# A hybrid decoder layer on Trainium2: the second output projection without gate/up products inside it

## The chip, the cores and the metric

The kernel runs on one core of a Trainium2 chip. The core has a matrix engine (TensorE, PE in the profile), a vector engine (VectorE, DVE), a scalar engine (ScalarE, ACT), a general engine (GpSimd, POOL) and a sync engine (SyncE, SP) that here issues most of the DMAs. TensorE multiplies a stationary operand of 128 by 128 with a moving one of up to 128 by 512 and writes into banks of an accumulation memory; the other engines read these banks. The metric is the device time of one execution in microseconds (us). The profile is one execution taken by the hardware profiler.

## What is computed

One decoder layer on 2048 tokens of 1024 channels. Cut to what matters here:

```python
hn = rms_norm(h, mix_pre_g)
proj = hn @ w_in                       # 1024 x 1792: conv input u, k, v, q
attn_out = sliding_window_attention(q, k, v, attn_sinks, rel_bias)   # window 128
conv_out = conformer_conv(u, ...)      # GLU, 31 causal taps, LayerNorm, silu, @ w_conv_pw
mixed = concatenate([attn_out, conv_out], axis=-1) @ w_out
h = h + rms_norm(mixed, mix_post_g)
hn = rms_norm(h, ffn_pre_g)
ff = (silu(hn @ w_gate) * (hn @ w_up)) @ w_down    # 1024 -> 2816 -> 1024
out = h + rms_norm(ff, ffn_post_g)
```

All inputs and outputs are float32. A product of two float32 matrices is made of three matmuls: each operand is split into a high part and a low part (the rest), and high by high, high by low and low by high are added up in one bank.

## The kernel before

**Tiles and stages.** The tokens go in four tiles of 512, numbered 0 to 3. A letter and a number name a stage, and every buffer's name carries it after an @ (without the number in the profile): A is the input projection of a tile, B its attention in four blocks of 128 tokens, C its convolution (taps on VectorE, then a tail: LayerNorm, silu and the pointwise product), W its output projection and norms. The feed-forward part works on pairs of tiles, (0, 1) and (2, 3), with a seven-product scheme of sums and differences: H makes the operands of a pair, F the gate and up products, G the down projection.

**Lanes and the planning clock.** The program is written out by a main stream and several lanes. Each stage is a generator that yields planned microseconds; `run` (line 1353) walks the main stage, adds what it yields to the planning clock `clk` and lets each lane issue as much work as its rate allows. A lane's item may have a condition (`needs`), tested on each pump, and items of one lane follow one another. `until` issues the rest of a lane's items up to a name at once. What is issued in this way has a priority in that order; the tile framework's scheduler then sets the order of the instructions on each engine, so that a later instruction can be placed ahead of an earlier one that is not ready. Lane `lc` issues the convolution taps at a lower priority and at a planned rate (0.4 for tile 2, 0.1 for tile 3 during F, 0.9 during G), `ld` the convolution tails of tiles 0 and 1, `lb` attention, `lh` the H stage.

**The output projection** (`stage_w`, line 697). The eight rows of `mixT` (0 to 3 from attention, 4 to 7 from the convolution) are taken in four groups of two. For a group, `acts` loads the two rows into buffers `at` (two of them) and splits them into `hl` (eight); for each half of the 1024 output columns, `weight` loads two blocks of `w_out` into `raw` (two buffers), splits them on ScalarE, and loads the low parts from `lo_out`, where the first projection has stored them. `block_half` (line 671) then does four banks of six matmuls each, planned at 1.3 us a bank, and adds each bank into `acc` (buffers `mid` for tile 1). So a group is 48 matmuls and W1 is 192. At the end `norm_w` (line 747) makes the residual, the norms, and the rows `hn_scr`; for tile 1 it is given to lane `lh` under the name N1.

**The stop in the second one.** W1 is run as the main stream with `ready=...`: after its second group (rows 2 and 3) it goes through the first `Q0` = 8 products of the F stage (`stage_pre`, line 887, with q from 0 to 7). Half-way, at the fifth, it issues the rest of tile 1's convolution tail (`ld.until("C1")`) and the operands of its third group. Each product is 12 matmuls of a 128-row block of w_gate or w_up with the operand B11 (tiles `x`), planned at 2.76 us; its result is stored to `keeps`. After W1, `stage_pre` goes on with q = 8 to 39: q = 8 to 19 with B11, and 20 to 39 with B21 on top of the kept results, which are loaded into `gb` (two buffers) and put into a bank by ScalarE (line 924) before the product.

**The first pair's operands.** `stage_h_plain` (line 829) makes B11 and B21 of a pair, four tiles each: a load of 512 tokens by 128 channels from `hn_scr`, four transposes on TensorE, scaling on ScalarE into `gb`, a store to `hT`, and the split. Before, both are put into `lh` without a condition as W1 starts, so they are issued beside its first half. `stage_pre` issues what is missing itself (line 935). S0 (`stage_h_sums`, line 842) makes the other operands from both tiles of the pair; it is gated by product 22 and the end of attention, and the taps are held until it has been issued.

Of the kernel before, what the change touches and what calls it, by code (L numbers as in the profile page):

```python
# [28 lines left out]
KC = D // P  # L29
# [8 lines left out]
def layer_kernel(ctx, tc, x, xT, cols, rows, sinks, relb, onehot, w_in, w_pw, w_out, w_gate, w_up, w_down, out):  # L38
# [8 lines left out]
    lab = ["X0"]  # L47
# [10 lines left out]
    def f4(tag, shape=(P, D)):  # L58
        return t_(tag, shape)

    def f2(tag, shape=(P, T)):
        return t_(tag, shape)

    def hl(tag):
        return t_(tag, (P, 2, T), F32R)
# [5 lines left out]
    def bank(tag, bufs):  # L71
        return ps.tile([P, T], F32, tag=tag, name=nm(tag), bufs=bufs)

    mm = lambda: bank("mm", 4)
# [65 lines left out]
    def weight(src, low, made, raw=None, on_pool=True):  # L140
        if raw is None:
            raw = t_("raw", (P, 2, T))
            nc.sync.dma_start(raw, src)
        return [split_w(raw[:, n], "w", low[n], made, on_pool) for n in range(2)]
# [526 lines left out]
    def block_half(acc, units, n, first, L, bank_of, s0=0):  # L671
        cs = slice(n * T, (n + 1) * T)
        for i in range(len(acc)):
            s = i + s0
            lab[0] = L
            o = bank_of()
            three(o, [((a[s // 4][:, 0, ss(s)], a[s // 4][:, 1, ss(s)]), (w[:, 0], w[:, 1])) for a, w in units])
            if first:
                act(acc[i][:, cs], o, AF.Copy)  # L679
            else:  # L680
                vtt(acc[i][:, cs], acc[i][:, cs], o, ALU.add)
            yield 0.65 * len(units)
# [11 lines left out]
            cs = slice(n * T, (n + 1) * T)  # L694
            tied(stt(acc[:, cs], acc[:, cs], r, gb[n], ALU.mult, ALU.mult))

    def stage_w(w, spill, G, atag, htag, mtag, bank_of, norm=None, ready=None):
        L = f"W{w}"
        lab[0] = L
        acc = [f4(atag) for _ in range(4)]  # L700

        def acts(gi, ms=None):
            aa = []
            for m in ms or load(gi):
                a = hl(htag)
                act(a[:, 0], m, AF.Copy)  # L706
                vtt(a[:, 1], m, a[:, 0].bitcast(F32), ALU.subtract)
                aa.append([a])
            return aa

        def load(gi):
            ms = []
            for c in range(G * gi, G * gi + G):
                ms.append(f2(mtag))
                nc.sync.dma_start(ms[-1], mixT[c, :, w * T : (w + 1) * T])
            return ms

        first = load(0)
        if w != 1:
            yield 5.0  # L720
            lab[0] = L
        nxt = acts(0, first)
        for gi in range(KC // G):
            aa = nxt
            for n in range(2):
                lab[0] = L
                if n == 0 and w != 1 and gi + 1 < KC // G:
                    rows_next = load(gi + 1)
                if n == 1 and gi + 1 < KC // G and not (ready and G * gi + G == 4):
                    nxt = acts(gi + 1, rows_next if w != 1 else None)  # L730
                ws = weight(w_out[2 * gi : 2 * gi + 2, :, n * T : (n + 1) * T].rearrange("c p t -> p c t"),
                            lo_out[n, 2 * gi : 2 * gi + 2], w > 0)
                yield from block_half(acc, list(zip(aa, ws)), n, gi == 0, L, bank_of)
            if ready and G * gi + G == 4:
                for i, c in enumerate(ready()):
                    if i == Q0 // 2:
                        ld.until("C1")
                        lab[0] = L
                        nxt = acts(gi + 1)
                    yield c  # L740
        tail = norm_w(w, spill, acc, mtag)
        if norm:
            norm(tail)
        else:
            yield from tail
# [54 lines left out]
    def lo(x, w, on_pool):  # L800
        (ptt if on_pool else vtt)(w[:, 1], x, w[:, 0].bitcast(F32), ALU.subtract)
# [9 lines left out]
    def turned(w, k, bank_of, tag):  # L811
        c = load_cols(w, k, tag)
        b = bank_of()
        for s in range(4):
            nc.tensor.transpose(b[:, s * P : (s + 1) * P], c[:, s], ident)
        return b
# [12 lines left out]
    def stage_h_plain(ws, ops, n, off):  # L829
        L = f"H{ws[0]}"  # L830
        for k in range(4):
            lab[0] = L
            b = turned(ws[0], k + off, tr, COLTAG[ws[0]][k] if ws[0] else "fa")
            u = f2("gb")
            act(u, b, AF.Copy, scale=g_ffn[:, k + off : k + off + 1])
            nc.scalar.dma_start(hT[ws[0] // 2][k + off], u)
            o = op_tile(ws, ops, n, k, {})
            act(o[:, 0], u, AF.Copy)
            lo(u, o, False)
            yield 2.0  # L840
# [46 lines left out]
    def stage_pre(ws, ops, mid, keep, q0=0, q1=None):  # L887
        PRE = PRES[ws[0]]
        q1 = q1 or 2 * PRE
        L = f"F{ws[0]}"  # L890
        raws = {}
        wops = {}
        kept = {}

        def load(q):
            if q < q1 and q % 2 == 0:
                lab[0] = L
                half, m = divmod(q, PRE)
                raw = t_("raw", (P, 2, T))
                for j in range(2):  # L900
                    src, pr = MATS[m + j]
                    nc.sync.dma_start(raw[:, j], src[2 * pr][:, half * T : (half + 1) * T])
                    raws[q + j] = raw[:, j]

        def fetch(q):
            if PRE <= q < q1:
                lab[0] = L
                kept[q] = f2("gb")
                nc.sync.dma_start(kept[q], keep[q - PRE])

        def split(q):
            if q < q1:
                lab[0] = L
                raw = raws.pop(q)
                wops[q] = split_f(raw, hl("w"))
                lo(raw, wops[q], ws[0] and q % 2 == 1)

        seeded = {}

        def seed(q):  # L920
            if PRE <= q < q1:
                lab[0] = L
                seeded[q] = mm()
                act(seeded[q], kept.pop(q), AF.Copy)  # L924

        load(q0)
        load(q0 + 2)
        for q in range(q0, q0 + 3):
            split(q)
        for q in range(q0, q1):  # L930
            half, m = divmod(q, PRE)
            started.add(f"P{ws[0]}.{q}")
            bn = "B21" if half else "B11"
            if len(ops.get(bn, ())) < 4:
                lh.until(f"{bn}.{ws[0]}")
            split(q + 3)
            load(q + 4)
            fetch(q + 2)
            lab[0] = L
            seed(q + 1)  # L940
            lab[0] = L
            o = seeded.pop(q) if half else mm()
            product(o, wops.pop(q), ops[bn], not half)
            if not half:
                u = f2("fa")
                act(u, o, AF.Copy)
                nc.scalar.dma_start(keep[m], u)
            else:
                if MATS[m][0] is w_gate:
                    sg = f2("fa")  # L950
                    act(sg, o, AF.Silu)
                else:
                    vtt(sg, sg, o, ALU.mult)
                    nc.sync.dma_start(mid[0, MATS[m][1]], sg)
            yield 2.76
# [316 lines left out]
    def since(lane, name, dt):  # L1272
        return name in lane.done and clk[0] >= lane.done[name] + dt
# [60 lines left out]
    NS = 12  # L1334
    AHEAD = 3
    PRES = {0: 20, 2: 16}
    Q0 = 8
    POOL_LO = (3, 6)
    PRE_S0, PRE_S2 = 22, 16
    H1, H2, H3, H4 = 0, 4, 7, 11  # L1340
    lb = Lane(RB, 0)
    lc = Lane(RC0, LC)
    lw = Lane(RW0, 0)
    lf = Lane(1.2, 0)
    lh = Lane(1.2, 0)
    lt = Lane(RT, 0)
    ld = Lane(2.0, 0)
# [5 lines left out]
    def run(gen):  # L1353
        for c in gen:
            clk[0] += c
            for lane in lanes:
                lane.pump(c)
# [53 lines left out]
    mids = [dr.tile([7, NF // 2, P, T], F32, name=f"mids{i}") for i in range(2)]  # L1411
    hT = [dr.tile([KC, P, T], F32, name=f"hT{i}") for i in range(2)]
    td = dr.tile([4, NF // 2, P, T], F32, name="td")
    keeps = [dr.tile([PRES[2 * i], P, T], F32, name=f"keeps{i}") for i in range(2)]
    ws, ops = (0, 1), {}
    for n, off in (("B11", 0), ("B21", 4)):
        lh.add(n + ".0", stage_h_plain(ws, ops, n, off))
    run(stage_w(1, True, 2, "mid", "hl", "at", mm, norm=lambda g: lh.add("N1", g), ready=lambda: stage_pre(ws, ops, mids[0], keeps[0], 0, Q0)))
    lc.hold = lambda: "S0" not in lh.done
    lh.until("B21.0")  # L1420
    lh.add("S0", stage_h_sums(ws, ops), lambda: f"P0.{PRE_S0}" in started and "B3" in lb.done)
    run(stage_pre(ws, ops, mids[0], keeps[0], Q0))
    lt.add("TS", stage_tsums(td))
    run(stage_p1(ws, ops, mids[0], keeps[0]))
    lt.until("TS")
# [2 lines left out]
    ws, ops = (2, 3), {}  # L1428
# [76 lines left out]
```

## Time and profile before

| what | value |
|---|---|
| three timed runs | 2012.16, 2020.62, 2017.57 us; median 2017.57 |
| span of the profiled execution, first to last instruction | 2016.4 us |
| granted TensorE clock, mean over the span | 0.991 |
| TensorE busy / VectorE busy / ScalarE busy | 1957.8 / 1489.5 / 985.7 us |
| HBM read and written | 330.60 MB and 119.02 MB |
| chain that ended last: TensorE / DMA / VectorE / ScalarE / issue | 38% / 5% / 3% / 1% / 1% of the span |

Only the instructions themselves lie in the span; the profiled execution's own time is not given beside it, so the span is compared with the median of the timed runs, which is 1.2 us longer. Busy time on TensorE counts pipelined matmuls whose ends are modelled: a matmul alone is listed at some 390 ns, and in a full stream the next begins 0.228 us later. In the rows of the timeline, the first two numbers are start and duration in us, then engine, line, operation, the tile written and the tiles read, shape and count; the bracket is the idle time of the engine just before, and what ended it. In the rows of windows, each engine has its busy time and in parentheses its instructions, then come the granted clock, the mean busy share of the DMA engines and GB/s. Helpers record many operations under one line (108 for matmuls, 85 for VectorE), so the names of the tiles tell the stages apart. In the rows of DMA issues, the size in KB of one and its median time from issue to landing end the row.

### The profile page before, as it was taken

The page shows a single profiled execution, that of the slowest core. Times are in us where ns is not written, and L with a number is a line of the kernel's source. Part 1 is how long each engine was busy: PE and PEld are TensorE (multiplying, and loading weights), DVE is VectorE, ACT ScalarE, POOL GpSimd, SP SyncE. Part 2 cuts the span into 40 slices and gives each one's busy share as a digit, 9 for nine tenths or more (in the row PEclk, how much of TensorE's full clock was granted, in tenths as well). Part 3 has the DMA queues.
Part 4 walks back from the last instruction along what each step waited for, and adds up shares of the span by engine and source line. Part 5 has one row for each costly group of instructions (what it writes and reads, how often), then busy time and mean ns, then how long its engine had stood idle before and what let it go on. Part 6 is the DMA issues. An engine that isn't in the chain of part 4 may idle for free. (4 is left out here: it accounts for less than half of the span.)

```text
span 2016.4 us, 27154 instructions
## 1 busy us (share of the span) xinstructions
PE 1957.8 (97%) x8826; PEld 1563.3 (78%) x8826; DVE 1489.5 (74%) x2679; ACT 985.7 (49%) x1938; POOL 355.0 (18%) x415
## 2 busy tenths in 40 slices
PE   8999999999998999999989999999899999999998
PEld 7877767677667778888878878778688888888886
DVE  5998987985794899888569984475766765545558
ACT  5455455457546633333355466456643343345543
POOL 6000223322110300000001022103523332221000
PEclk9999999999999999999989999999999999999999
DMA  8786645669559878777476778579944443366654
GB/s 309 267 298 221 207 148 175 194 228 322 180 178 325 281 238 269 253 253 254 149 239 216 238 261 283 173 262 348 333 159 167 157 160 107 107 238 214 200 187 162
DMA packets 234110, 451.44 MB, mean 224 GB/s; under 512 B 23496, under 2 KB 49264, under 8 KB 233968
## 3 DMA queue, kind: packets, MB, share of 16 engines
q1 hardware_dynamic: 211184, 411.96, 60.9%
q10 hardware_dynamic: 20544, 30.42, 4.1%
q0 software_dynamic: 2240, 7.34, 0.9%
q8 instruction: 69, 1.13, 0.2%
q14 instruction: 73, 0.60, 0.1%
HBM read 330.60 MB, written 119.02 MB: 223 GB/s over the span
## 5 line engine op out<-in xcount | busy, mean ns | idle before, releaser
L85 DVE SCALAR_TENSOR_TENSOR fc@C<-glu@C,colt,fc@C 128x512 f32<-128x512 f32 x480 | 367.8, 780 | 3.0
L108 PE MATMUL mm@F<-hl@H,w@F 128*128 128x512 f32 x1056 | 254.9, 392 | 5.3 <-ACT mm@F L924 4.9
L108 PEld LDWEIGHTS mm@F<-hl@H,w@F 128*128 128x128 f32 x1056 | 198.5, 189 | 48.8 <-ACT mm@F L924 6.7
L108 PE MATMUL mm@G<-hl@G,hl@G 128*128 128x512 f32 x924 | 228.0, 396 | 6.4 <-DVE x@G L85 4.3
L108 PE MATMUL mm@A<-hl@A,w@A 128*128 128x512 f32 x840 | 206.3, 396 | 3.0 <-ACT hl@A L318 1.2
L108 PEld LDWEIGHTS mm@G<-hl@G,hl@G 128*128 128x128 f32 x924 | 174.1, 190 | 44.5 <-issue 4.1
L797 ACT ACTIVATE w@F<-chl@F 128x512 fp32r<-128x512 f32 x220 | 135.6, 625 | 135.3 <-PE mm@F L108 123.3
L108 PE MATMUL mm@G<-w@G,hl@G 128*128 128x512 f32 x876 | 199.5, 389 | 0.0
L108 PEld LDWEIGHTS mm@G<-w@G,hl@G 128*128 128x128 f32 x876 | 164.4, 188 | 34.1
L108 PEld LDWEIGHTS mm@A<-hl@A,w@A 128*128 128x128 f32 x840 | 154.7, 188 | 39.4 <-DVE hl@A L85 3.0
L85 DVE TENSOR_TENSOR w@F<-chl@F,w@F 128x512 fp32r<-128x512 f32 x198 | 144.9, 733 | 34.7 <-ACT w@F L797 34.3
L108 PE MATMUL mm@F<-mid@H,w@F 128*128 128x512 f32 x528 | 131.1, 393 | 7.4 <-ACT mm@F L924 7.2
L108 PE MATMUL mm@F<-p@H,w@F 128*128 128x512 f32 x528 | 129.1, 389 | 0.8 <-ACT at@F L1046 0.8
L108 PE MATMUL mm@F<-ql@H,w@F 128*128 128x512 f32 x528 | 127.2, 389 | 0.7 <-ACT w@F L797 0.7
L108 PE MATMUL mm@F<-x@H,w@F 128*128 128x512 f32 x528 | 125.5, 391 | 0.0
L108 PEld LDWEIGHTS mm@F<-mid@H,w@F 128*128 128x128 f32 x528 | 98.3, 188 | 30.2 <-ACT mm@F L924 9.0
L108 PEld LDWEIGHTS mm@F<-p@H,w@F 128*128 128x128 f32 x528 | 98.9, 188 | 21.9 <-ACT at@F L1046 1.4
L108 PEld LDWEIGHTS mm@F<-ql@H,w@F 128*128 128x128 f32 x528 | 99.0, 188 | 21.6 <-ACT w@F L797 1.1
L108 PEld LDWEIGHTS mm@F<-x@H,w@F 128*128 128x128 f32 x528 | 98.7, 188 | 21.0
L108 PE MATMUL tr@W<-w@W,ql@W 128*128 128x512 f32 x384 | 103.0, 408 | 8.4 <-ACT ql@W L706 5.1
L133 ACT ACTIVATE w@A<-raw@A 128x512 fp32r<-128x512 f32 x110 | 67.7, 626 | 78.8 <-PE mm@A L108 51.5
L108 PE MATMUL mm@W<-w@W,hl@W 128*128 128x512 f32 x384 | 101.5, 404 | 2.2 <-ACT x@W L679 0.7
(302 smaller groups left out, 3337.0 us busy)
## 6 DMA issues: line engine op xcount, KB each, us to landing
mids<-fa@F SPq DMA_DIRECT2D x154, 256.0 KB, 2.7
raw@A<-w_in SPq DMA_DIRECT2D x55, 512.0 KB, 4.4
w@A<-lo_in SPq DMA_DIRECT2D x84, 256.0 KB, 3.5
fc@G<-mids SPq DMA_DIRECT2D x77, 256.0 KB, 3.5
fa@G<-mids SPq DMA_DIRECT2D x75, 256.0 KB, 4.5
gb@F<-keeps SPq DMA_DIRECT2D x72, 256.0 KB, 4.3
raw@W<-w_out SPq DMA_DIRECT2D x32, 512.0 KB, 5.5
w@W<-lo_out SPq DMA_DIRECT2D x48, 256.0 KB, 4.4
```

The lines of the kernel that those rows point to most:

```text
L85: r = op(*args, **kw)
L108: r = nc.tensor.matmul(*args, **kw)
L133: act(w[:, 0], raw, AF.Copy)
L797: act(w[:, 0], x, AF.Copy)
```

## The change

W1 has no stop any more: its four groups follow one another, and the rest of tile 1's convolution tail is issued, where it is not yet, ahead of the operands of the third group, in the second half of the second group. The F stage does all its 40 products in one go behind W1. B11 and B21 of the first pair get a condition: their lane items begin only when `NH` = 24 planned microseconds have passed since W0 was issued to its end. The call that issued the rest of B21 after W1 is gone; `stage_pre` does that where it needs it.

```diff
-    def stage_w(w, spill, G, atag, htag, mtag, bank_of, norm=None, ready=None):
+    def stage_w(w, spill, G, atag, htag, mtag, bank_of, norm=None):
...
-                if n == 1 and gi + 1 < KC // G and not (ready and G * gi + G == 4):
+                if n == 1 and gi + 1 < KC // G:
+                    if w == 1 and G * gi + G == 4:
+                        ld.until("C1")
+                        lab[0] = L
                     nxt = acts(gi + 1, rows_next if w != 1 else None)
                 ws = weight(w_out[2 * gi : 2 * gi + 2, :, n * T : (n + 1) * T].rearrange("c p t -> p c t"),
                             lo_out[n, 2 * gi : 2 * gi + 2], w > 0)
                 yield from block_half(acc, list(zip(aa, ws)), n, gi == 0, L, bank_of)
-            if ready and G * gi + G == 4:
-                for i, c in enumerate(ready()):
-                    if i == Q0 // 2:
-                        ld.until("C1")
-                        lab[0] = L
-                        nxt = acts(gi + 1)
-                    yield c
...
-    Q0 = 8
...
+    NH = 24
...
     for n, off in (("B11", 0), ("B21", 4)):
-        lh.add(n + ".0", stage_h_plain(ws, ops, n, off))
-    run(stage_w(1, True, 2, "mid", "hl", "at", mm, norm=lambda g: lh.add("N1", g), ready=lambda: stage_pre(ws, ops, mids[0], keeps[0], 0, Q0)))
+        lh.add(n + ".0", stage_h_plain(ws, ops, n, off), lambda: since(lw, "W0", NH))
+    run(stage_w(1, True, 2, "mid", "hl", "at", mm, norm=lambda g: lh.add("N1", g)))
     lc.hold = lambda: "S0" not in lh.done
-    lh.until("B21.0")
     lh.add("S0", stage_h_sums(ws, ops), lambda: f"P0.{PRE_S0}" in started and "B3" in lb.done)
-    run(stage_pre(ws, ops, mids[0], keeps[0], Q0))
+    run(stage_pre(ws, ops, mids[0], keeps[0]))
```

## The prediction

> **What bounds the kernel now.** I read the page first, then the windows around the second output projection, then the waits and the order of TensorE in them.
>
> ```profile
> span 2016.4 us, 27154 instructions
> PE 1957.8 (97%) x8826; PEld 1563.3 (78%) x8826; DVE 1489.5 (74%) x2679; ACT 985.7 (49%) x1938; POOL 355.0 (18%) x415
> ```
>
> TensorE is busy 97% of the span, so work that changes place on it costs nothing by itself; only TensorE's gaps and its slow stretches can shrink or grow. All gaps together are 2016.4 - 1957.8 = 58.6 us. The share that this edit can reach lies in the stretch from the start of W1 (472) to the first use of the S0 operands (693.5):
>
> ```profile
> core 0: us, PE busy (x) PEld busy (x) DVE busy (x) ACT busy (x) POOL busy (x), PEclk, DMA share, GB/s
> 472.00:533.00 61.00, 56.95 (x272) 39.02 (x270) 33.31 (x93) 39.73 (x90) 9.87 (x12) 0.97 0.66 231
> 533.00:559.60 26.60, 26.60 (x128) 20.15 (x127) 23.42 (x55) 13.00 (x35) 2.38 (x2) 1.00 0.61 202
> 559.60:594.00 34.40, 29.90 (x142) 21.40 (x141) 34.19 (x63) 15.20 (x39) 3.25 (x4) 1.00 0.53 173
> 594.00:635.00 41.00, 40.55 (x179) 33.23 (x178) 26.27 (x45) 26.92 (x47) 7.52 (x24) 1.00 0.77 271
> 635.00:670.00 35.00, 29.49 (x133) 23.28 (x134) 21.32 (x31) 23.56 (x43) 9.83 (x7) 0.95 0.95 326
> ```
>
> The gaps are 4.05 us in the first half of W1, none while the eight products run, 4.50 us in its second half, 0.45 us in N1's stretch and 5.51 us where S0 loads its operands: 14.5 us in all. The order of TensorE names their causes (a bracket is the idle time before the row):
>
> ```profile
> 495.29 0.50 PE L108 MATMUL mm@W<-w@W,hl@W 128*128 128x512 f32 x1
> ...
> 506.96 0.66 PE L815 MATMUL tr@H<-ident,fa@H 128*128 128x128 f32 x4 [2.52 <-ACT gb@H L835]
> ...
> 513.65 5.70 PE L108 MATMUL mm@W<-w@W,hl@W 128*128 128x512 f32 x24
> ...
> 533.16 3.06 PE L108 MATMUL mm@F<-x@H,w@F 128*128 128x512 f32 x12
> ...
> 577.91 0.66 PE L500 MATMUL tr@B<-ident,p@B 128*128 128x128 f32 x4 [3.36 <-DVE p@B L85]
> ...
> 593.59 32.80 PE L108 MATMUL mm@F<-x@H,w@F 128*128 128x512 f32 x144
> ...
> 637.31 7.36 PE L108 MATMUL mm@F<-hl@H,w@F 128*128 128x512 f32 x24 [2.75 <-ACT mm@F L924]
> ...
> 646.36 5.76 PE L108 MATMUL mm@F<-hl@H,w@F 128*128 128x512 f32 x24 [1.70 <-ACT mm@F L924]
> ```
>
> The clock adds to it:
>
> ```profile
> 508.00:510.00 2.00, 1.70 (x5) 0.55 0.67 243
> 510.00:512.00 2.00, 2.00 (x7) 0.60 0.03 8
> 578.00:580.00 2.00, 2.00 (x11) 1.00 0.44 126
> 638.00:640.00 2.00, 2.00 (x7) 0.50 1.01 386
> 640.00:642.00 2.00, 2.00 (x8) 0.67 1.05 404
> ```
>
> After the gaps of 2.52 and 2.75 us the granted clock fell for some 4 us, a loss of (0.45 + 0.40) x 2 = 1.7 us each; after the 3.36 us gap it stayed at 1.00. So the gaps and the clock together are 14.5 + 3.4 = 17.9 us, which is all that the edit could ever win in this stretch. [...]
>
> **The change, part by part.** *The eight products* (q 0 to 7) leave W1 and stand at the head of the F stage. At 32.80/144 = 0.228 us a matmul they are 96 x 0.228 = 21.9 us of TensorE, which are paid there instead: 0. With each goes one ACT split, one DVE low part, one eviction, one weight load on SP and one store of the kept product on ACT's queue; these move too, past W1's own loads of w_out, its low parts and mixT, which then come sooner after one another. The F stage has 40 products either way, and S0 is tied to product 22, so S0 and the first use of its operands stay where they are after W0.
>
> *The transposes.* B11 and B21 of the first pair (eight tiles) may start only 24 planner microseconds after W0 is issued, at best inside W1's third weight group (each half group is four steps of 1.3, so 20.8 for the first two groups). This is a gate in the planning, no wait on the chip; behind it in the same lane stand N1 and S0.
>
> ```profile
> 486.42 2.04 SPq L793 DMA_DIRECT2D fa@H<-hn_scr  x4
> 512.83 1.14 ACT L706 ACTIVATE hl@W<-at@W 128x512 fp32r<-128x512 f32 x2
> 517.11 0.69 DVE L85 TENSOR_TENSOR hl@H<-gb@H,hl@H 128x512 fp32r<-128x512 f32 x1 [1.64 <-ACT hl@H L838]
> 526.40 0.33 ACTq L631 DMA_DIRECT2D mixT<-fc@C  x1
> ```
>
> Now they take 486.42 to 517.8, and W1's operands for its second group are split on ACT only at 512.83, behind them. With them gone the 2.52 us gap, its 1.7 us of clock, and the 1.5 us left of that window have no cause there: between -5.7 and 0. They come again in the second half, so I take -3. At lane rate 1.2 the eight need 16/1.2 = 13.3 planner us, 24 to 37.3 of W1's 41.6, so B11 should be ready before the first product.
>
> *The cover.* The 26.6 us window without any gap goes out of W1. Its third group needs the convolution's first two columns, its fourth the last two, stored at 526.40. Landing, load, split and low part after that:
>
> ```profile
> w@W<-lo_out SPq DMA_DIRECT2D x12, 256.0 KB, 2.9
> raw@W<-w_out SPq DMA_DIRECT2D x5, 512.0 KB, 5.5
> ...
> fa@H<-hn_scr SPq DMA_DIRECT2D x8, 256.0 KB, 5.1
> hT<-gb@H ACTq DMA_DIRECT2D x8, 256.0 KB, 3.0
> ...
> mixT<-fc@C ACTq DMA_DIRECT2D x4, 256.0 KB, 2.6
> ...
> at@W<-mixT SPq DMA_DIRECT2D x4, 256.0 KB, 3.0
> ...
> 440.00:480.00 40.00, 40.00 (x182) 29.26 (x180) 22.99 (x42) 30.41 (x51) 15.50 (x41) 1.00 0.98 346
> ```
>
> The last columns are usable at 526.4 + 2.6 + 3.0, and with a split of 0.57 and a low part of 0.69 at 533.3, some 534 with queueing. From 495.3, the end of W1's first group, to 513.65 TensorE did 18.4 - 4.0 of gaps - 5.3 for the transposes (32 at 0.66/4) = 9.1 us of attention and convolution, and to 533.16 another 19.5 - 10.9 = 8.6; with W1's second and third groups (10.9 each) that is 39.5, so it asks for the fourth group at 534.8, or at 526.2 if 8.6 us of attention lag behind. The wait is 0 by the one and 7.8 by the other; I take +2, nearer to the first, since attention's place does not change.
>
> *The DMA in W1's second half.* Groups three and four load 4 x 0.5 MB of weights, 8 x 0.25 MB of low parts and 4 x 0.25 MB of mixT, 5 MB; the transposes 8 x 0.25 in and 8 x 0.25 out, 4 MB; attention and the first product weights 1.5 MB. 10.5 MB at the 346 GB/s of a window at share 0.98 are 30.3 us, and TensorE has 21.9 us of W1 and some 8 us of attention beside them: no slack, where today this half runs at share 0.53. I take +3, from 0 (weights loaded ahead) to +8. The 4.5 us of gaps that are there today come from attention (waiting for the DVE) and stay: 0, from -4.5 to +4.
>
> *N1* is finished 21.9 us sooner against products 20 to 32. Today its stores reach hn_scr just before S0 loads from it (the first of four each):
>
> ```profile
> 630.24 0.33 ACTq L785 DMA_DIRECT2D hn_scr<-mid@W  x1
> 643.10 0.43 SPq L793 DMA_DIRECT2D fc@H<-hn_scr  x1
> ```
>
> TensorE waits for seeds (ACT L924) while DMA is at share 0.95. Without them the 5.51 + 1.7 us may shrink; S0's own loads stay. From -7.2 to 0, I take -3.
>
> *The convolution taps of the third tile* run beside W1 at 0.4 us per planner us, and are then held until S0 is issued. 22.1 planner us fewer in W1 are 8.8 us, or 12 taps, not done there.
>
> ```profile
> 472.00:594.00 122.00, 37.72 (x52) 0.99 0.61 208
> 800.00:900.00 100.00, 11.17 (x15) 1.00 0.74 251
> 690.31 0.32 SPq L574 DMA_DIRECT2D y_scr<-fc@C  x1
> 773.89 0.37 SPq L574 DMA_DIRECT2D y_scr<-fc@C  x1
> 1332.36 32.67 PE L108 MATMUL mm@G<-hl@G,hl@G 128*128 128x512 f32 x132 [3.93 <-DVE x@G L85]
> ```
>
> A tap is 37.72/52 = 0.73 us. From 690.31 to 773.89 one channel's 31 taps took 2.7 us each, so the third tile ends 12 x 2.7 = 32 us later, and the fourth, which then goes at 15 per 100 us, has 5 taps less done when the down projection starts. There 0.9 applies: 5 x 0.73/0.9 = 4 us late for the fourth projection, which ends close before the 3.93 us gap at 1332. I take +2, from 0 to +5.
>
> **Sum.** -3 + 2 + 3 + 0 - 3 + 2 = +1 on 2016.4: a span of 2017. The three timed runs have a median of 2017.57, 1.2 above the profiled span; with that the forecast is 2018. Its own range is 2008 to 2028.
>
> **The rivals.** One row more is needed for them:
>
> ```profile
> 491.60 0.62 ACT L797 ACTIVATE w@F<-raw@F 128x512 fp32r<-128x512 f32 x1
> ```
>
> (a) *Slower: W1 starves at its joints.* The convolution's products stay 10 to 12 us apart as their shared buffers allow, while W1's second group runs at once: the fourth group waits its 7.8 us; the transposes then share full DMA queues with W1's weights (+8), and the first product waits. It decides once the last convolution store is still near 526 while W1 wants its fourth group before 530. Its upper ends are 8 + 8 = 16, with -3 - 3 + 2 beside them +12 on the forecast's base, with the clock about 2030. For it: the window that DMA fills at 346 GB/s, and that the cover is without a gap today. Against it: attention and products of F may fill the holes. (b) *Faster: the crowd at 495 to 513 and the one at 635 are both gone.* -5.7 - 7.2 with the costs at 0: -12.9, 2005. For it: the two largest gaps after attention's are in these places. Against it: the transposes' work is only moved, and S0's loads remain. (c) *The change does not do what it says:* an engine's order is made from priorities, and a weight split for F is made at 491.60, 40 us before the first product; if the scheduler draws products up into W1 again, the time stays at 2017. That asks for ready transposes, which are late now. (d) *The late taps hit harder:* if the fourth projection is what ends last before 1332, all 12 taps count, 8.8/0.9 = 10 us: +11, 2028.
>
> **How the numbers follow.** Forecast 0.42, (c) 0.08: both within 0.5% (10 us, about what a measurement of this kernel can tell), so 0.50. (a) 0.25 and (d) 0.06 make 0.31 slower; (b) 0.19 faster. The predicted time is the forecast's. The range 2004 to 2032 reaches to (b) and (a) and leaves out about 0.1 on each side, where more than one joint opens or both gains come in full.
>
> **What would show it.** mm@W without mm@F from its first to its last matmul, W1 ending near 560 to 575; hl@W's second split well before 512; the transposes near 520 to 550 with DMA share above 0.9 there; gaps of mm@W before the fourth group (wrong if over 8 us); the seeds' waits at 635 to 670 at about half of 5.5 us (wrong if unchanged); the store of the third tile's last channel some 30 us after 773.89; the gap at 1332 larger by 2. It is wrong as a whole if the stretch up to the first S0 operand moves by more than 10 us.

## The result and the profile after

| | before | after |
|---|---|---|
| median of 20 runs, us | 2017.87 | 2022.97 |
| lowest and highest, us | 2008.93 and 2025.18 | 2016.23 and 2030.43 |
| span of the profiled execution, us | 2016.4 | 2028.2 |

The ratio of after to before is 1.0026, with a 95% interval from 1.0013 to 1.0038: 5.1 us more, resolved, and inside the 0.5% that the prediction counts as no change. The profiled execution of after is one of its longest (2029.90 us against a median of 2022.97), so its 11.8 us over before must not be read as the effect. To separate the two, both kernels were profiled a second time (below), and each execution is cut at four places on TensorE that all kernels have: the last matmul of the input projection, the first with an S0 operand (`ql@H`), the first of the first G, and the first of the last G. I call the three parts the head (W1, N1, S0, the 40 first products), the long stretch (the other F products of the first pair), and the rest. TensorE's order ahead of the head is the same before and after, and the end behind the last cut took 221.5 to 221.9 us in each kernel.

The page of after, the lines that answer to those of before:

```profile
span 2028.2 us, 27158 instructions
PE 1963.1 (97%) x8826; PEld 1565.9 (77%) x8826; DVE 1493.6 (74%) x2679; ACT 985.8 (49%) x1938; POOL 358.5 (18%) x415
```

The windows of these three parts, before:

```profile
core 0: us, PE busy (x) PEld busy (x) DVE busy (x) ACT busy (x) POOL busy (x), PEclk, DMA share, GB/s
472.40:693.60 221.20, 206.69 (x951) 156.13 (x950) 160.19 (x316) 134.60 (x280) 40.34 (x52) 0.98 0.72 246
693.60:1006.40 312.80, 309.90 (x1361) 254.19 (x1360) 261.57 (x421) 119.60 (x214) 0.00 (x0) 1.00 0.71 237
1006.40:1794.80 788.40, 765.50 (x3377) 627.95 (x3376) 528.26 (x812) 389.78 (x702) 184.71 (x184) 0.99 0.63 213
```

And after, with the same columns:

```profile
475.30:701.50 226.20, 210.95 (x950) 159.06 (x949) 146.62 (x299) 134.05 (x279) 39.27 (x56) 0.96 0.71 239
701.50:1021.10 319.60, 310.85 (x1362) 253.98 (x1361) 269.99 (x435) 119.49 (x214) 0.00 (x0) 1.00 0.69 234
1021.10:1806.60 785.50, 764.96 (x3377) 627.32 (x3376) 533.52 (x815) 389.58 (x701) 189.48 (x184) 0.99 0.62 214
```

The head is 5.0 us longer, the long stretch 6.8 us, the rest 2.9 us shorter; the remaining 2.9 us were lost ahead of the head, where nothing was changed, and are chance. In the long stretch VectorE has 14 instructions more (435 against 421) in 8.4 us more of busy time: the taps. TensorE's gap there goes from 2.9 to 8.75 us. The second profiles, before and then after, show less of a difference in the same stretch, 5.4 us of gaps against 7.05:

```profile
691.70:1007.70 316.00, 310.57 (x1362) 254.21 (x1361) 260.82 (x420) 119.69 (x214) 0.00 (x0) 1.00 0.71 235
695.90:1014.30 318.40, 311.35 (x1362) 255.53 (x1361) 268.92 (x433) 119.60 (x214) 0.00 (x0) 0.99 0.71 234
```

The order of TensorE after, where it waits in the head and in the long stretch (the bracket is the idle time before the row):

```profile
525.18 3.02 PE L108 MATMUL mm@W<-w@W,hl@W 128*128 128x512 f32 x12 [1.04 <-ACT hl@W L706]
...
554.61 4.37 PE L108 MATMUL mm@W<-w@W,hl@W 128*128 128x512 f32 x11 [2.87 <-ACT hl@W L706]
...
571.74 19.46 PE L108 MATMUL mm@F<-x@H,w@F 128*128 128x512 f32 x85
...
603.66 24.82 PE L108 MATMUL mm@F<-x@H,w@F 128*128 128x512 f32 x108 [1.20 <-ACT fa@F L942]
...
640.80 7.10 PE L108 MATMUL mm@F<-hl@H,w@F 128*128 128x512 f32 x24 [2.89 <-ACT mm@F L920]
...
848.25 1.66 PE L108 MATMUL mm@F<-yt@H,w@F 128*128 128x512 f32 x6 [1.57 <-DVE gb@F L85]
...
884.40 0.73 PE L108 MATMUL mm@F<-ql@H,w@F 128*128 128x512 f32 x2 [2.38 <-ACT w@F L793]
```

W1 has no F products in it and ends at 571.7; the wait of 2.52 us on the transposes is gone, two waits on W1's own operands have come (1.04 and 2.87), and the largest wait on a kept product is what it was (2.89, before 2.75).

### The profile page after: what moved, and what is told of

It reads as the page before. It is cut to its first block, busy times and chain, and to the rows that moved or that the text cites. A ratio compares the mean times of both kernels' runs of the same rounds, so it can differ in the third digit from the quotient of the medians.

```text
span 2028.2 us, 27158 instructions
## 1 busy us (share of the span) xinstructions
PE 1963.1 (97%) x8826; PEld 1565.9 (77%) x8826; DVE 1493.6 (74%) x2679; ACT 985.8 (49%) x1938; POOL 358.5 (18%) x415
## 4 chain that ended last, share of the span: by engine, by line
PE 48%; DMA 10%; DVE 7%; ACT 2%; issue 2%; SPq 0%; DVEq 0%; ACTq 0%
PE mm@F L108 27%; PE mm@G L108 17%; PE tr@W L108 3%; DVE fc@C L85 1%; DVE w@F L85 1%; DMA at@W<-mixT 1%; DMA mids<-fa@F 1%; DMA fc@G<-w_down 1%; DVE hl@G L85 1%; DVE fa@F L85 1%; DVE chl@F L85 1%; DMA chl@F<-w_gate 1%; DMA td<-fc@G 1%; DMA mb@G<-td 1%; DMA wx@G<-w_down 1%
## 5 line engine op out<-in xcount | busy, mean ns | idle before, releaser
L108 PE MATMUL mm@W<-w@W,hl@W 128*128 128x512 f32 x384 | 106.7, 416 | 5.3 <-ACT hl@W L706 4.3
```

What stands on the lines that cost most here:

```text
L108: r = nc.tensor.matmul(*args, **kw)
```

## The experiments

Twelve runs, in three groups. Ratios are to the kernel before, run on the same chip beside each group. The stage lengths are each from one profile; the taps are VectorE's instructions on `glu@C` in the long stretch.

| kernel | ratio, 95% interval | head | long stretch | rest | taps in the long stretch |
|---|---|---|---|---|---|
| before | 1 | 221.2 | 312.8 | 788.4 | 68 |
| before again (e11) | 0.9997, 0.9984 to 1.0010 | 220.5 | 316.0 | 788.1 | 68 |
| after | 1.0026, 1.0013 to 1.0038 | 226.2 | 319.6 | 785.5 | 81 |
| after again (e8) | 1.0010, 0.9989 to 1.0030 | 223.2 | 318.4 | 784.7 | 80 |
| e1 no gate | 1.0047, 1.0033 to 1.0061 | 226.5 | 319.2 | 789.8 | 79 |
| e2 taps kept | 0.9997, 0.9986 to 1.0009 | 220.2 | 313.3 | 791.1 | 66 |
| e3 before, taps cut | 1.0011, 0.9997 to 1.0025 | 225.7 | 315.3 | 788.9 | 78 |
| e4 no gate, taps kept | 0.9982, 0.9968 to 0.9996 | 215.2 | 313.7 | 785.9 | 69 |
| e12, the same again | 0.9984, 0.9971 to 0.9997 | 216.2 | 314.7 | 790.9 | 68 |
| e5 taps thin | 1.0090, 1.0061 to 1.0119 | 220.7 | 319.2 | 800.5 | 71 |
| e6 no gate, more taps | 1.0051, 1.0032 to 1.0070 | 220.3 | 325.6 | 789.8 | 53 |
| e7 before, more taps | 1.0050, 1.0031 to 1.0070 | 229.8 | 319.6 | 780.8 | 55 |
| e9 before, no sums | 0.9985, 0.9972 to 0.9999 | 230.5 | 308.1 | 786.9 | 67 |
| e10 after, no sums | 0.9980, 0.9966 to 0.9994 | 223.1 | 311.6 | 782.8 | 81 |

**The gate of the transposes (e1).** The kernel after with the condition taken away:

```diff
-        lh.add(n + ".0", stage_h_plain(ws, ops, n, off), lambda: since(lw, "W0", NH))
+        lh.add(n + ".0", stage_h_plain(ws, ops, n, off))
```

> The kernel after the change, but with the transposes of the first pair free to begin as W1 starts (no gate of 24 planned us). Theory (what costs is the missing stop and the taps that come later by it, the gate is neutral): ratio to before 1.0015 to 1.004, as after the change; the stretch from the first matmul with an S0 operand to the first of G stays near the 319.6 us of after. Rival (the gate costs, since the transposes now share W1's second half): ratio 0.999 to 1.001, and W1's gaps of about 5 us before its fourth group and at the attention gone.

Measured 1.0047, above both expectations: with the taps late the gate does not cost, it helps, since without it the time is longer still (after has 1.0026 and 1.0010). The long stretch is that of after (319.2), and the rest is 4 to 5 us longer (789.8).

**The taps (e2, e3).** e2 is the kernel after, and e3 the one before, with another planned rate while W1 runs:

```diff
+    lc.rates["T2"] = 0.61        # e3: 0.26
     run(stage_w(1, ...))
+    lc.rates["T2"] = RC2
```

> The kernel after the change, but the convolution taps of the third tile are planned at 0.61 us per planned us while W1 runs (0.4 x 63.7 / 41.6), so that as many are issued by W1's end as before the change. Theory (the late taps fill VectorE in the long stretch of F and make TensorE wait there): that stretch falls from 319.6 to 313 to 315 us, the store of the third tile's last channel returns from 821 to about 780, and the ratio to before is 1.0005 +- 0.001. Rival (the loss is in W1 and the head of F): the long stretch stays within its noise, the ratio is 1.0025 or more.

> The kernel before the change, stop and early transposes as they were, but the taps of the third tile are planned at 0.26 us per planned us while W1 runs (0.4 x 41.6 / 63.7), so that as few are issued by W1's end as after the change. Theory (late taps cost): ratio 1.0015 to 1.003, the long stretch of F goes from 312.8 to 317 or more. Rival (the loss is in W1 and the head of F, or is the clock's): ratio 0.999 to 1.001 and the long stretch at 312 to 314.

e2 is as expected by the theory: 0.9997, the long stretch back at 313.3, the last store of the third tile at 767.34 where after has it at 821.58. So the loss goes away when the taps are issued as early as before, though the stop is still missing. The head became shorter too (220.2), which the theory did not say, and the rest longer (791.1). e3 is the test the other way round, and it does not bear the theory out: it has 78 taps in the long stretch, nearly as many as after, but its ratio is 1.0011 with an interval that holds 1, and its long stretch of 315.3, where 317 or more was expected, lies between the two of before (312.8 and 316.0).

**Stop alone (e4, e12).** e1 and e2 together, so that the stop is gone and the transposes and the number of taps are as before; e12 is the same file again.

> The kernel after the change without the gate of the transposes and with the taps at 0.61 while W1 runs: only the stop is gone. Theory (late taps cost, stop and gate are neutral): ratio 0.999 to 1.001. Rival 1 (the cover of the eight products is what is lost): 1.0015 or more. Rival 2 (the stop was harmful and only the gate and the taps hid it): 0.998 or less.

> The kernel after the change without the gate and with the taps at 0.61 while W1 runs, once more: the only one so far below before. If that was no chance: ratio 0.997 to 0.9995, long stretch 313 to 314 us, head 213 to 219. If it was: 0.9995 to 1.001.

0.9982 and 0.9984, both intervals below 1: just short of the second rival's 0.998, and outside the theory's range. Of the kernels that leave out no work it is the fastest tried, 0.17% below before, and below after by 0.3 to 0.4% (0.9982 against 1.0010 and 1.0026). The gain is in the head (215.2 and 216.2). Its windows in the first of the two profiles:

```profile
471.20:686.40 215.20, 207.49 (x950) 155.57 (x949) 157.94 (x316) 135.09 (x280) 40.26 (x50) 0.99 0.75 252
686.40:1000.10 313.70, 310.12 (x1362) 254.33 (x1361) 262.52 (x421) 119.63 (x214) 0.00 (x0) 1.00 0.70 238
```

TensorE's gaps in the head are 7.7 us where before has 14.5 and after 15.25, and the waits for kept products have a large part in that. They are 1.5 us in all (line, releaser, us in total, times, longest):

```profile
PE mm@F L108 <- ACT mm@F L920: 1.5, 4, 0.5
```

against this in after:

```profile
PE mm@F L108 <- ACT mm@F L920: 5.2, 3, 2.9
PE mm@W L108 <- ACT hl@W L706: 3.9, 2, 2.9
PE mm@F L108 <- ACT fa@F L942: 2.2, 2, 1.2
```

In e12 they are 2.1 us. Why these loads come in time there was not tried.

**How full VectorE is (e5, e6, e7).** If the late taps simply filled VectorE, thinner taps or fewer of them in the long stretch should shorten it. e5 is after with `lc.rates["T2"] = 0.2` ahead of `run(stage_p1(...))`; e6 is e1 with a rate of 1.0 during W1; e7 is before with 0.61.

> The kernel after the change, but in the long stretch of F the taps of the third tile are planned at 0.2 us per planned us instead of 0.4, so that the ones that are late are spread thinner. Theory (VectorE is too full at the head of the long stretch, where the late taps run at the pace of one per product): the long stretch falls from 319.6 to 312 to 315 us, the head stays at 226, and the ratio to before is about 1.000 unless the G stage pays for the taps that are then missing (up to +4 us, 1.002). Rival (it is the number of taps in the stretch, or the clock, not their density): the long stretch stays at 318 or more, ratio 1.0025.

> The kernel after the change without the gate, taps of the third tile at 1.0 us per planned us while W1 runs. Theory (earlier taps are worth some 0.25% until VectorE is full beside W1 and the head of F): long stretch at 312 to 314 us, ratio 0.996 to 0.999. Rival (the gain with 0.61 was only the way back to the load of before, and more taps crowd N1 and S0): 1.000 or more, head 3 us or more longer than with 0.61 (215.2).

> The kernel before the change, with its stop and early transposes, taps of the third tile at 0.61 us per planned us while W1 runs. If the stop itself is neutral and only the place of the taps counts, it gains like the kernel without stop: ratio 0.997 to 0.999. If the stop costs what the taps at 0.61 without it gained (0.9982), or the taps are already early enough here: 0.9995 to 1.001.

All three went against the theory; e6 came out as its rival said, and the ratios of e5 and e7 lie outside both of their expectations. e5 left the long stretch at 319.2 and lost 15 us more in the rest, where the fourth tile's missing taps hold the fourth projection up: it ends at 1346.7, where after has 1319.5, and TensorE waits 17.8 us in three gaps at the transposes behind it. e6 and e7 have only 53 and 55 taps in the long stretch, and it is longer than with 68 (325.6 and 319.6). e7 loses as much in the head (229.8), 8.3 us of it in one wait for a kept product. So the loss does not follow the number of taps nor their density. The rate of 0.61, the best of those tried without the stop, costs 0.5% in the kernel before, where 0.4 is better.

**The side work (e9, e10).** In both profiles of after TensorE waits at the same instruction, some 180 us into the long stretch (2.38 and 3.16 us), and not in those of before. These are the queue of SP, its wait at the store (us in total, times, longest), VectorE and ScalarE there, in after (855 to 890), one fence for each:

```profile
869.44 0.86 SPq L1083 DMA_DIRECT2D wx@G<-w_down  x2
870.39 0.86 SPq L1083 DMA_DIRECT2D fc@G<-w_down  x2
...
874.98 1.63 SPq L1089 DMA_DIRECT2D td<-wx@G  x2
...
878.64 0.42 SPq L999 DMA_DIRECT2D gb@F<-keeps  x1
```

```profile
SPq L1089 <- DVE wx@G L85: 6.0, 4, 3.2
```

```profile
870.29 0.69 DVE L85 TENSOR_TENSOR chl@F<-raw@F,chl@F 128x512 f32<-128x512 f32 x1
874.26 0.69 DVE L85 TENSOR_TENSOR wx@G<-wx@G 128x512 f32<-128x512 f32 x1 [3.29 <-DMA wx@G<-w_down]
```

```profile
873.64 0.62 ACT L793 ACTIVATE w@F<-chl@F 128x512 fp32r<-128x512 f32 x1
883.20 0.60 ACT L1028 ACTIVATE mm@F<-gb@F 128x512 f32<-128x512 f32 x1 [8.94 <-DMA gb@F<-keeps]
```

The lane that makes the differences of w_down for G (`stage_tsums`) has its four loads issued together; VectorE stands 3.29 us at the first subtraction, which nothing needs soon; the store of its result stands at the head of SP's queue meanwhile (the wait of 3.2 us), and the load of the kept product comes behind it. ScalarE waits 8.94 us for that load, and the weight split behind it is what TensorE waits for (the row at 884.40). The second profile of after has the same chain:

```profile
874.82 0.60 ACT L1028 ACTIVATE mm@F<-gb@F 128x512 f32<-128x512 f32 x1 [10.72 <-DMA gb@F<-keeps]
```

e9 and e10 are before and after without this side work:

```diff
-    lt.add("TS", stage_tsums(td))
+    lt.add("TS", iter(()))
...
-            return td[{2: 1, 3: 2, 4: 3, 5: 0}[ty], pr]
+            return w_down[2 * pr + ty % 2, :, 0:T]
```

> The kernel before the change without the differences of w_down that lane lt makes beside the long stretch of F (44 loads, 44 subtractions, 44 stores left out; the down projection reads w_down itself in their place, so its output is another). Base line for the next one: long stretch 308 to 313 us.

> The kernel after the change, with the same left out. Theory (the late taps push this side work into places where its loads hold VectorE and SP's queue, and a load of a kept product comes late behind it, as at 870 to 884 of the profile): without the side work the long stretch is as long as in the kernel before without it, within 2 us, and below 314. Rival (the late taps cost by themselves, whatever else runs): it stays 5 us or more longer than there.

Without it the long stretch of after falls from 319.0 (mean of two) to 311.6 and that of before from 314.4 to 308.1. The head and the long stretch, e9 first:

```profile
473.20:703.70 230.50, 208.57 (x950) 156.88 (x949) 165.03 (x319) 134.58 (x280) 41.89 (x51) 0.98 0.72 239
703.70:1011.80 308.10, 308.10 (x1362) 254.95 (x1362) 235.29 (x374) 121.37 (x214) 0.00 (x0) 1.00 0.50 163
471.70:694.80 223.10, 209.37 (x950) 158.59 (x949) 149.22 (x298) 134.21 (x279) 39.38 (x52) 0.97 0.73 244
694.80:1006.40 311.60, 308.55 (x1361) 254.78 (x1360) 245.69 (x391) 120.45 (x215) 0.00 (x0) 1.00 0.50 164
```

The difference is 3.5 us where it was 4.6: less than the rival's 5, more than the theory's 2, and each number of e9 and e10 is one profile, where two profiles of before differ by 3.2. So neither came true, and by these profiles most of the difference is there without the side work. The two kernels take the same time (2018.26 against 2020.66 us, ratios 0.9980 and 0.9985 with intervals that overlap almost wholly), but this does not speak for the theory. The edit also changed SP's order ahead of the long stretch, from 614 us on in e9 and from 596 on in e10, and the head of e9 is 9 to 10 us longer than that of before, with 12.0 us of waits for kept products. By these profiles e9 loses more in its head than e10 does in the long stretch. The side work also takes DMA time in the whole long stretch (its share falls from 0.71 to 0.50 without it), so the pair does not test the one chain.

**The profiles again (e8, e11).**

> The kernel after the change once more, on this chip, for its ratio beside the others and a second profile. Expected: ratio 1.0015 to 1.004; long stretch 317 to 320 us, head 223 to 227, if the late taps cost what the first profile shows; a long stretch near 313 would mean that the first profile was an outlier.

> The kernel before the change once more, for a second profile of its stages. If the long stretch is set by the order of the instructions: 312 to 314 us again, against 319.6 and 318.4 of the two profiles of after; the head varies by some 3 us (221). If it is chance: 316 or more. Ratio 0.999 to 1.001.

The long stretch of after came out at 318.4, as expected; that of before at 316.0, at the edge of what was to be called chance. The ratio of 1.0010 is lower than expected; its interval holds 1.0026, and 1 as well. With the means of two profiles each, the change is +3.9 us in the head, +4.6 in the long stretch and -3.2 in the rest: +5.3, beside 5.1 in the medians of the timed runs. Some 1.7 us of the head's 3.9 is chance, a clock that fell in one profile of after and not in the other (last section).

## Why the prediction was right, and where its steps were not

The forecast of no change (2018 us, 2008 to 2028) holds 2022.97, and no rival came true; the nearest is the one of the late taps, in another place and at half its price. Of the forecast's own six terms one was right, one right only in part, one right in size for another reason, and three were wrong. That the sum still came within 5 us is luck: the errors are small and of both signs. (The +11 of rival (d) counts the taps' own +2 beside the 10 that take its place; it is +9.)

- **The eight products, 0:** right. They stand behind W1 and are paid there.
- **The transposes, -3:** right for the gaps. That of 2.52 us is gone, and beside the moved transposes only waits of 0.45 and 0.24 us came. All gaps of W1 went from 8.6 us (121.0 - 112.45) to 6.1; the rows are W1 and the two parts of the head behind it:

```profile
475.50:571.70 96.20, 90.07 (x421) 62.35 (x420) 58.36 (x163) 53.67 (x125) 13.91 (x18) 0.95 0.62 204
571.70:632.30 60.60, 58.45 (x257) 46.04 (x257) 44.32 (x74) 38.21 (x79) 8.89 (x26) 1.00 0.75 262
632.30:701.50 69.20, 62.24 (x273) 50.47 (x272) 43.94 (x62) 42.17 (x77) 16.28 (x12) 0.95 0.81 269
```

The clock took the gain back: 0.95 over the 96.2 us of W1 is some 5 us lost, the same in the second profile, where before lost 1.7 and in its second profile some 3.5. And the gate's worth has no fixed sign. With the taps late, e1 without it is slower than after; with the taps early, e4 and e12 without it have a head 4 to 5 us shorter than e2 (215.2 and 216.2 against 220.2).

- **The cover, +2:** the size is right (1.04 + 2.87 us), the cause is not. ScalarE's queue shows the last column of the convolution stored at 535.74; this store took 5.1 us, so it was in memory near 541. The last load of W1's fourth group left SP's queue only at 549.25:

```profile
535.74 0.33 ACTq L631 DMA_DIRECT2D mixT<-fc@C  x1
...
546.84 0.38 ACTq L529 DMA_DIRECT2D mixT<-at@B  x1
...
553.93 0.63 ACT L706 ACTIVATE hl@W<-at@W 128x512 fp32r<-128x512 f32 x1 [3.23 <-DMA at@W<-mixT]
```

SP's queue there, and what it waited for (us in total, times, longest):

```profile
547.90 0.37 SPq L846 DMA_DIRECT2D chl@H<-hT  x1
549.25 0.32 SPq L715 DMA_DIRECT2D at@W<-mixT  x1
```

```profile
SPq L846 <- DMA hT<-gb@H: 5.1, 1, 5.1
...
SPq L715 <- DMA mixT<-at@B: 0.8, 1, 0.8
```

SP stood 5.1 us at an early load of S0, which waits for the transposes' stores, and the load for W1 was behind it. But this is not what ended last: SP then waited another 0.8 us for the attention store issued at 546.84, which frees the load's buffer. The second profile of after has the same wait (0.8 us). In e4, whose transposes are early, SP waits at that load for the same release, with no load of S0 ahead of it:

```profile
SPq L715 <- DMA mixT<-at@B: 5.6, 1, 5.6
```

So this load goes by a buffer that W1 shares with attention, and not by the last column of the convolution, which the prediction went by. That the moved transposes made the wait is not shown: in e1, with early transposes, W1 still waits 3.7 us for these operands.
- **DMA in W1's second half, +3:** wrong. I asked for a share above 0.9 at 520 to 550; there it is 0.64, and over W1's second half (523.6 to 571.7) 0.51. The sum of 10.5 MB over 30 us was too short in time, since that half with its attention took 48 us.
- **N1 earlier, -3:** wrong. The waits for kept products are 5.2 and 4.6 us in the two profiles of after, 4.9 and 4.3 in those of before. N1's last store to hn_scr is issued at 627.93 in after, 10 us ahead of the largest of these waits, where before has it at 634.88, as that wait begins; so the wait does not need N1's stores beside it. S0's loads moved up with N1 (the first comes 8 us behind the last store, before and after), so the two were not taken apart. What makes the kept products late is not shown. A new wait came, for ScalarE's evictions into `fa` (2.2 us).
- **The taps, +2:** the step that failed. The count was right (12 late, measured 13 and 12; the third tile's end 32 us late, measured 48 and 42 by the two pairs of profiles). But the prediction let them cost in G, "4 us late for the fourth projection", and nothing in the long stretch. The gap at 1332 grew only from 3.93 to 4.64 us, and from 3.83 to 5.27 in the second profiles. The rest, G among it, did not become longer (785 against 788), and the long stretch pays 4.6. In it TensorE is the bound (busy 310.85 of 319.60 us in after), and VectorE and SP go through their instructions in the same order in both profiles of a kernel: the late taps changed which instruction stands ahead of which, and part of the price is in waits like the one at 884.

So the forecast was right because its costs and gains were small and of both signs; the way of the largest one was not foreseen. That the planned rate of the taps decides over the loss is clear in e4 and e12 against e1 (0.65%). Of e2 against after it is clear by the first measurement of after (1.0026) and not by the second (1.0010). That late taps cost by their lateness is not shown: e3 has as many of them late and no clear loss, and with fewer of them in the long stretch e6 and e7 are slower. A new rate gives all engines a new order, and the gain of e2 and e4 may be that of a luckier order. How it costs is shown for one wait; e9 and e10 leave 3.5 of the 4.6 us unexplained.

## What to carry to other kernels

When a piece of the main stream is taken out of a stage, ask what was paced by it: here a background lane was planned per microsecond of that stage, and 22 planned microseconds less pushed its work into a later stretch, which became longer. After such a change try the lane's rate again before the change is judged; with that the same edit without its gate went from 0.47% slower to 0.17% faster. The rate does not carry over: 0.61 cost the kernel before 0.5%, and 1.0 cost the edit as much. And cut two profiles of each kernel at the same instructions before explaining a few microseconds.

## What the runs showed that was not expected

In the first of the two profiles of after, TensorE's granted clock fell in a stretch without any gap. At the start of W1, matmuls of 128 rows, listed at some 0.50 us, alternate with attention matmuls of 64 rows, listed at 0.38 us:

```profile
480.00:484.00 4.00, 4.00 (x12) 0.91 1.02 385
484.00:488.00 4.00, 4.00 (x9) 0.50 0.85 308
488.00:492.00 4.00, 4.00 (x21) 0.74 0.53 142
```

TensorE counts as busy throughout (4.00 us in each of the three windows), and by these clocks it loses (0.09 + 0.50 + 0.26) x 4 = 3.4 us. In the 20 us from 5 us behind the start of the head, the granted clock was 0.83 in the profiles of after and e1, 0.91 in that of e6, and 1.00 in the eleven others, the second profile of after among them. So 0.17 x 20 = 3.4 us come and go by chance, which is part of the spread of single runs and of the head of after. What lowers the clock there is not shown by any run.
